# Order of copies and background transfers in the gate stage of a two-group mixer layer

## The chip, the core and the metric

The kernel runs on one NeuronCore of a Trainium2 chip. The core has a matrix engine (TensorE, PE in the profile; its weight loads are listed apart as PEld), a vector engine (DVE), a scalar engine (ACT), GpSimd (POOL) and SyncE (SP). Each of them works through its own list of instructions in order, and semaphores hold them to each other. Transfers are issued by SP and by POOL, onto two different queues, and run on the same 16 DMA engines. The metric is the device time of one execution in microseconds, the median of several runs.

## What is computed

One layer of a diffusion backbone runs for 128 prompt tokens and for 512 sample tokens; the kernel takes the 640 tokens together. The part that matters here is the gated merge of four branches:

```python
proj = h @ lw['w_in']
y_a = a_b * dwconv3(a_c * a_x, lw['conv_a_w'], lw['conv_a_b'])
...
g_a, g_b, g_c, g_d = jnp.split(jax.nn.sigmoid(h @ lw['w_gate'] + lw['b_gate']), N_BRANCH, axis=-1)
merged = (g_a * (y_a @ lw['w_br_a']) + g_b * (y_b @ lw['w_br_b'])
          + g_c * (y_c @ lw['w_br_c']) + g_d * (y_d @ lw['w_br_d']))
return merged @ lw['w_o'], kh, vh, s_f, s_b
```

Here `h` is 640 x 1024, each `y` is 640 x 256, and `merged` is 640 x 1024. Around it stand the input projection, an HGRN scan, neighbourhood attention and a gMLP before, and the output projection, a second norm and a convolutional feed-forward (1024 to 5632, and 2816 back to 1024) behind.

## The kernel before, in words

Everything is float32. A product in float32 is made of three products of a rounded type: each operand is split into a high part (an ACT copy that rounds) and a low part (a DVE subtraction of the high part from the original), and high x high, high x low and low x high are added up in PSUM. So each weight tile and each operand needs a copy on ACT and a subtraction on DVE before the matrix engine can use it.

The gate stage takes 16 *pairs*, numbered 0 to 15 (`p_`): four branches in the order d, a, b, c, with four output tiles each. A pair covers two output tiles of 128 features and all 640 tokens in two halves of 320. It is computed as a two-by-two block product with seven products instead of eight (numbers 1 to 7), so sums of weight blocks and of operand blocks are needed as well. `gprod` issues one of the seven for the gate (12 matmuls), and `bprod` one for the branch (3 matmuls): 105 matmuls of 128x128 by 128x320 in a pair. What a pair needs beside them:

- Weight units `A`, `B`, `C`, `Z` (tiles `w`, `B`, `S` in the profile): `g_a`/`g_al`, `g_b`, `g_c`, `g_zh`/`g_zl` make their high and low parts. `B` is made from the sums in `gx["S"]`, which is half of the region `D`. For pairs 0 to 2 these sums were made by earlier transfers and lie in memory as `gsum`; `g_s01` loads them (`D<-gsum`, on POOL). From pair 3 on `g_s01` adds them on DVE.
- Banks of PSUM (`m`, one bank; `g`, two banks): product 1 lands in one bank and is copied to another on ACT, since two products build on it (`oact(b3, b1)` in `g_pair`, and `oact(p3_, p1_)` for the branch). The sums of the seven products are put together on ACT and DVE in the tiles `ga`, `gb` and `y`, and the gate goes through a sigmoid on ACT (`g_sig`).
- The branch operand `y`: in the second pair of a branch (pairs 1, 5, 9; `n0 == 1`) `y_load` brings the next branch's operand into `gx["Y"]`, the other half of region `D`: SP loads the high part, and POOL adds the low part by an accumulating transfer, which must wait for the first one. At the end of the same pair `y_sums` makes the operand sums from it on DVE (four subtractions and additions, `D<-D`), and `y_split` splits these in the branch's first pair. The operand is `ydd` for branch d, the tile `A` for branch a, and `ybd` and `ycd` in memory for branches b and c.

The order of the gate stage is written out by hand: while `fixed[0]` is set, the engines take `ovec`, `oact`, `opool` and `omm` instructions in the order of the source. What stands before that (input projection, attention) is placed by a scheduler.

Branch a's operand is finished in `evac_in`, in the last tile of the input projection, as half of the tile `YA` (`MG` in the profile). `split_y("A", ...)` splits it there: one ACT copy and one DVE subtraction of 128x1280.

Background transfers: `down_sums` is a list of 72 steps, each one transfer on POOL (`usum`, then `wsum`), which make sums of feed-forward weights in memory, many of them accumulating. `g_all` issues 5 of them ahead of each pair. POOL's list is in order, so a step issued ahead of a pair stands ahead of that pair's `D<-gsum`, of its accumulating transfer for `y`, and of the loads of finished operands (`E<-ybd`, `A<-ycd`).

Of the kernel before, what the change touches and what calls it, by code (L numbers as in the profile page):

```python
# [10 lines left out]
F32R = mybir.dt.float32r  # L11
U8 = mybir.dt.uint8
AF = mybir.ActivationFunctionType
# [3 lines left out]
P = 128  # L17
# [29 lines left out]
T = 640  # L47
# [22 lines left out]
def tile_step(ctx: ExitStack, tc: tile.TileContext, a: dict, outs: list, dbg=None):  # L70
# [58 lines left out]
    def region(tag, shape, dt=F32):  # L129
        return big.tile(shape, dt, tag=tag, name=nm(tag))  # L130
# [25 lines left out]
    ovec, opool, oact = Ordered(nc.vector), Ordered(nc.gpsimd), Ordered(nc.scalar).activation  # L156
# [51 lines left out]
    for x in LORD.split():  # L208
        if x[0] == "w":
            i, h = int(x[1]), int(x[2])  # L210
# [180 lines left out]
    R = {}  # L391
# [6 lines left out]
    def evac_in(sec, n, ps):  # L398
        psv = None if isinstance(ps, list) else ps[:, :, 0:HC]
        if sec in ("ff", "fb"):  # L400
            d = 0 if sec == "ff" else 1
            ff = need("A", "FF", [P, 2, 2, T])
            kk = need("B", "KK", [P, 2, 2, T])
            if psv is None:
                for c in range(2):
                    cs = slice(c * HC, (c + 1) * HC)
                    act(ff[:, d, n, cs], ps[c], AF.Sigmoid)
                    act(kk[:, d, n, cs], ps[c], AF.Sigmoid, scale=-1.0)
            else:
                act(c2(ff[:, d, n]), psv, AF.Sigmoid)  # L410
                act(c2(kk[:, d, n]), psv, AF.Sigmoid, scale=-1.0)
            i = d * 2 + n
            vec.tensor_scalar(ff[:, d, n], ff[:, d, n], oml[:, i:i + 1], lb[:, i:i + 1],
                              ALU.mult, ALU.add)
            vec.tensor_scalar(kk[:, d, n], kk[:, d, n], oml[:, i:i + 1], None, ALU.mult)
        elif sec == "q":
            dd = need("D", "HD", [P, 2560])
            act(c2(dd[:, n * T:(n + 1) * T]), psv, AF.Silu)
        elif sec == "g":
            o = need("MG1", "HO", [P, 2560])  # L420
            act(c2(o[:, 1280 + n * T:1280 + (n + 1) * T]), psv, AF.Silu)
        elif sec == "du":
            x0 = need("X0", "DX0", [P, 2560])
            act(c2(x0[:, n * T:(n + 1) * T]), psv, AF.Copy)
        elif sec in ("ac", "ax", "ab"):
            if (sec, n) == ("ac", 0):
                drain(lambda: "hgrn_out" in R)
            y = need("MG0", "YA", [P, 2, 2, T])
            if sec == "ac":
                act(c2(y[:, 0, n]), psv, AF.Copy)  # L430
                return
            if sec == "ab":
                drain(lambda: "conv" in R)
            x = y[:, 0 if sec == "ax" else 1, n]
            vec.tensor_tensor(c2(x), psv, c2(x), ALU.mult)
            if (sec, n) == ("ab", 1):
                drain(lambda: "ada39" in R)
                R["ya"] = split_y("A", y[:, 1].rearrange("p n t -> p (n t)"))
        elif sec in ("ck", "cq", "cv"):
            if sec == "cv":  # L440
                dst = need("G", "CG", [P, 1280])[:, n * T:(n + 1) * T]
            else:
                f = need("F", "CF", [P, 2560])
                o = 0 if sec == "ck" else 1280
                dst = f[:, o + n * T:o + (n + 1) * T]
            sc = 0.125 if sec == "cq" else 1.0
            cg, cw = (4, 16) if sec == "cq" else (8, 8)
            dv = dst[:, 0:TS].rearrange("p (g r c) -> p r g c", g=cg, r=8)
            for (b, r0, r1) in ((0, 0, 5), (1, 5, 8)):
                src = ps[:, b, 0:(r1 - r0) * 64].rearrange("p (r g c) -> p r g c", g=cg, c=cw)  # L450
                act(dv[:, r0:r1], src, AF.Copy, scale=sc)
            act(dst[:, TS:T], ps[:, 1, 192:320], AF.Copy, scale=sc)
# [220 lines left out]
    def split_y(tag, y):  # L673
        w = region(tag, [P, 2, 2, T], F32R)
        wf = w.rearrange("p h k t -> p h (k t)")
        act(wf[:, 0], y, AF.Copy)
        vec.tensor_tensor(wf[:, 1], y, wf[:, 0].bitcast(F32), ALU.subtract)
        return w
# [472 lines left out]
    def low(w, x, h):  # L1151
        ovec.tensor_tensor(w, x, h.bitcast(F32), ALU.subtract)
# [25 lines left out]
    def g_b(p_, lows=None):  # L1178
        b = gw[p_, "B"] = gunit(p_, 1)
        oact(b[:, 0], gx["S"], AF.Copy)  # L1180
        if lows is None:
            low(b[:, 1], gx["S"], b[:, 0])
        else:
            lows.append((b[:, 1], gx["S"], b[:, 0]))
# [23 lines left out]
    def gprod(o, p_, i, first):  # L1208
        u, n = GPROD[i]
        w = gw[p_, u]  # L1210
        xh_, xl_ = gx["x"][i]
        for k in range(4):
            for j, (h, x) in enumerate(((0, xh_), (0, xl_), (1, xh_))):
                omm(o, w[:, h, n, k, :], x[:, k, :], start=(first and k == 0 and j == 0),
                   stop=(k == 3 and j == 2), skip_group_check=True)
            tick(0.44)
# [19 lines left out]
    def g_sig(p_, i, o, x):  # L1236
        bi, n = gp_id(p_)
        gc = C_BG + GI[BR[bi]] * 8 + n + 4 * i
        oact(o, x, AF.Sigmoid, bias=p1[:, gc:gc + 1])
# [24 lines left out]
    def g_pair0(r):  # L1264
        gx["bi"] = 0
        bank = [pm() for i in range(4)]
        R["mo"] = bank[2]
        b1, b3, b2, b4 = [m[:, 0:HC] for m in bank]
        ga = gw[0, "gt", 0] = gp.tile([P, T], F32, tag="gt", name=nm("ga"))
        gb = gw[0, "gt", 1] = gp.tile([P, T], F32, tag="gt", name=nm("gb"))  # L1270
        ps = gw[0, "ps"] = pg()
        p1_, p3_ = ps[:, 1, 0:HC], ps[:, 0, 0:HC]
        gprod(b1, 0, 1, True)
        oact(ga[:, 0:HC], b1, AF.Copy)
        bprod(p1_, 0, 1, True)
        oact(p3_, p1_, AF.Copy)
        gprod(b3, 0, 2, True)
        ovec.tensor_tensor(ga[:, 0:HC], b3, ga[:, 0:HC], ALU.add)
        g_sig(0, 0, ga[:, 0:HC], ga[:, 0:HC])
        bprod(p3_, 0, 2, False)  # L1280
        drain(lambda: "Y1" in gx)
        gprod(b4, 0, 4, True)
        g_split(3, gx["t3"])
        g_s01(1, r[1])
        gprod(b1, 0, 6, False)
        oact(gb[:, 0:HC], b1, AF.Copy)
        g_a(1, r[1])
        y_sums()
        gprod(b2, 0, 5, True)
        ovec.tensor_tensor(gb[:, 0:HC], b2, gb[:, 0:HC], ALU.subtract)  # L1290
        gx["C"] = region("MG1", [P, 2, 3, HC], F32R)
        lows, x3 = y_split()
        oact(x3[2], x3[1], AF.Copy)
        gprod(b1, 0, 7, False)
        oact(gb[:, HC:T], b1, AF.Copy)
        for x in lows + [x3]:
            low(*x)
        ovec.tensor_tensor(ga[:, HC:T], b4, gb[:, HC:T], ALU.add)
        g_sig(0, 0, ga[:, HC:T], ga[:, HC:T])
        ovec.tensor_tensor(gb[:, HC:T], b2, gb[:, HC:T], ALU.subtract)  # L1300
        r[2] = gp_load(2)
        gprod(b3, 0, 3, True)
        g_al(1, r[1])
        y = gw[0, "y"] = gp.tile([P, T], F32, tag="gt", name=nm("y"))
        c2_ = gw[0, "b2"] = pm()[:, 0:HC]
        bprod(p1_, 0, 6, False)
        oact(y[:, 0:HC], p1_, AF.Copy)
        ovec.tensor_tensor(gb[:, 0:HC], b3, gb[:, 0:HC], ALU.add)
        bprod(c2_, 0, 5, True)
        bprod(p1_, 0, 7, False)  # L1310
        oact(y[:, HC:T], p1_, AF.Copy)
        ovec.tensor_tensor(y[:, HC:T], c2_, y[:, HC:T], ALU.subtract)
        g_s23(1, r[1])
        gx["Y"] = gx["Y1"]

    def g_pair(p_, r):
        n, q = p_ + 1, p_ - 1
# [18 lines left out]
            g_zl(p_, r[p_])  # L1336
        gprod(b1, p_, 1, True)
        g_sig(q, 1, gw[q, "gt", 1], gw[q, "gt", 1])
        oact(b3, b1, AF.Copy)
        g_close(q)  # L1340
        ps = gw[p_, "ps"] = pg()
# [1 line left out]
        bprod(p1_, p_, 1, True)  # L1343
        oact(p3_, p1_, AF.Copy)
        if not q:
            g_b(p_)
            late = g_c(p_, r[p_])
            g_zh(p_, r[p_])
        g_merges(q)
# [29 lines left out]
        y = gw[p_, "y"] = gp.tile([P, T], F32, tag="gt", name=nm("y"))  # L1379
# [42 lines left out]
    def g_all(r):  # L1422
        drain(lambda: "gx3" in R and "last" in R)
        r[1] = gp_load(1)
        fixed[0] = True
        sums_ = down_sums()
        g_pair0(r)
        for p_ in range(1, GPAIR + 1):
            for _ in range(5):
                next(sums_, None)  # L1430
            if p_ == GPAIR:
                fixed[0] = False
                for j in range(GATES + 1, GATES + 3):
                    ld[j] = units[j][0]()
                    rd[j] = units[j][1](ld[j])
            g_pair(p_, r)
        m_split(2)
        m_split(3)
# [1216 lines left out]
```

## Time and profile before

| what | us |
|---|---|
| median of 3 runs | 999.44 |
| lowest and highest run | 998.62, 1199.35 |
| the profiled execution, whole | 999.27 |
| its span, first to last instruction | 997.5 |
| pair 1 begins, pair 15 ends (about) | 290, 524 |

The prediction is made against the profiled execution, 999.27 us. Its span is 997.5 us, so 1.77 us lie around the span. It is 0.17 us below the median of the three runs.

How rows are read. A row of the timeline has the start in us, the duration in us, the engine, the line, the operation, output<-input by the program's names, partitions x elements, and a count where equal instructions follow each other (then the duration is that of the group); in brackets stands the time that the engine had been idle before, and what released it. Most calls in the gate stage go through the helper at line 150, so a line tells little and the tile names tell more. SPq and POOLq rows are issues of transfers. A row of the list of transfers has the size of one in KB and the time from issue to landing in us. A row of the waits has the engine and what it waited for, the total in us, the number of times and the longest. A row of the windows has, for each engine, busy time and in brackets the number of instructions, then the granted clock of TensorE, the DMA engines' busy share and GB/s.

### The profile page before, as it was taken

To read this page: it belongs to the slowest core of one execution; us is meant where nothing else is said; L and a number is where in the kernel's file an instruction comes from. 1 tells how busy PE (TensorE), PEld (TensorE's weight loads), DVE (VectorE), ACT (ScalarE), POOL (GpSimd) and SP (SyncE) were. 2 spreads that over 40 slices of the span, in tenths; PEclk is the share of its full clock that TensorE was granted. 3 is DMA by queue.
4 is the path that set the end of the run, shared out by engine and by line. 5 is a ranking of instruction groups with operands and counts; after the bars stand their busy time and mean duration, and the time that the engine had idled before them with its cause. 6 is when DMAs were issued, how large, how long until landed. Compare 5 with 4: busy or idle time off the path is not lost.

```text
span 997.5 us, 19012 instructions
## 1 busy us (share of the span) xinstructions
PE 984.5 (99%) x7437; PEld 931.6 (93%) x7437; DVE 861.9 (86%) x1411; ACT 592.5 (59%) x1034; POOL 199.9 (20%) x272
## 2 busy tenths in 40 slices
PE   8999999999999999999999999999999999999997
PEld 6899999999989999999998899999999999888886
DVE  6679899878978789888877788999999998999796
ACT  6652343445575565555655376877777777756672
POOL 1000023414123131333200021222222222100004
PEclk9999999999999999999999999999999999999999
DMA  9886349898189799999939785766666666976742
GB/s 356 334 287 245 124 139 299 217 261 275 54 274 259 200 291 268 251 287 301 229 138 349 261 301 156 216 167 169 176 169 163 177 170 193 362 256 230 279 134 105
DMA packets 76858, 227.54 MB, mean 228 GB/s; under 512 B 10561, under 2 KB 25441, under 8 KB 74081
## 3 DMA queue, kind: packets, MB, share of 16 engines
q1 hardware_dynamic: 44832, 149.91, 42.1%
q0 software_dynamic: 31936, 76.43, 32.5%
q8 instruction: 58, 0.95, 0.4%
q14 instruction: 32, 0.25, 0.1%
HBM read 185.26 MB, written 61.36 MB: 247 GB/s over the span
## 4 chain that ended last, share of the span: by engine, by line
PE 85%; DVE 6%; DMA 5%; issue 1%; ACT 1%; POOL 1%; SPq 0%; POOLq 0%; DVEq 0%
PE g L1723 21%; PE m L150 20%; PE m L2186 9%; PE g L374 9%; PE m L1723 5%; PE g L150 4%; PE m L1475 4%; PE g L2186 4%; PE g L955 2%; PE g L1475 1%; PE m L539 1%; DMA D<-hdr 1%; PE m L1718 1%; DMA D<-ycd 1%; DMA ybd<-D 1%
## 5 line engine op out<-in xcount | busy, mean ns | idle before, releaser
L374 PE MATMUL g<-XH,w 128*128 128x320 f32 x576 | 140.5, 318 | 0.0
L374 PEld LDWEIGHTS g<-XH,w 128*128 128x128 f32 x576 | 98.7, 188 | 2.3 <-issue 1.0
L150 PE MATMUL m<-XH,w 128*128 128x320 f32 x416 | 98.9, 311 | 1.1 <-ACT gb L150 0.6
L374 PE MATMUL g<-XL,w 128*128 128x320 f32 x288 | 89.1, 309 | 0.0
L150 PEld LDWEIGHTS m<-XH,w 128*128 128x128 f32 x416 | 70.8, 188 | 3.1 <-ACT gb L150 0.8
L150 PE MATMUL m<-XL,w 128*128 128x320 f32 x208 | 63.0, 310 | 0.0
L2186 PE MATMUL m<-w,XH 128*128 128x512 f32 x246 | 58.5, 390 | 0.0
L2186 PEld LDWEIGHTS m<-w,XH 128*128 128x128 f32 x246 | 46.1, 188 | 9.5
L374 PEld LDWEIGHTS g<-XL,w 128*128 128x128 f32 x288 | 54.2, 188 | 0.3 <-issue 0.2
L150 ACT ACTIVATE w<-raw 128x640 fp32r<-128x640 f32 (+3 forms) x53 | 48.6, 931 | 2.6 <-DMA raw<-in_w_in_dram 1.5
L150 DVE TENSOR_TENSOR w<-raw,w 128x640 fp32r<-128x640 f32 (+3 forms) x47 | 48.5, 1048 | 1.9 <-ACT w L150 1.9
L150 POOL DMA_DIRECT2D wsum<-in_w_dn_dram x36 | 37.2, 1215 | 48.7 <-issue 34.2
L150 DVE SCALAR_TENSOR_TENSOR X<-MG,p2t,X 128x641 f32<-128x641 f32 x44 | 38.9, 883 | 1.0 <-ACT X L150 0.2
L150 DVE SCALAR_TENSOR_TENSOR X<-X,p2t,X 128x641 f32<-128x641 f32 x44 | 38.9, 884 | 0.9
L150 PEld LDWEIGHTS m<-XL,w 128*128 128x128 f32 x208 | 38.6, 188 | 0.6 <-issue 0.6
L1723 PE MATMUL g<-XL,w 128*128 128x320 f32 x240 | 38.6, 310 | 0.0
L1723 PE MATMUL g<-XL,C 128*128 128x320 f32 x240 | 38.3, 309 | 0.0
L150 ACT ACTIVATE gb<-m 128x320 f32<-128x320 f32 x32 | 14.0, 436 | 40.7 <-PE m L150 40.7
L1723 PEld LDWEIGHTS g<-XL,w 128*128 128x128 f32 x240 | 36.0, 188 | 0.6 <-ACT MG L150 0.3
L1723 PEld LDWEIGHTS g<-XL,C 128*128 128x128 f32 x240 | 36.0, 188 | 0.0
L150 ACT ACTIVATE X<-X,p2t 128x641 f32<-128x641 f32 x22 | 20.4, 927 | 18.4 <-DVE X L150 18.4
L150 ACT ACTIVATE X<-g 128x320 f32<-128x320 f32 x30 | 13.1, 437 | 30.6 <-PE g L1723 30.6
(622 smaller groups left out, 2946.3 us busy)
## 6 DMA issues: line engine op xcount, KB each, us to landing
wsum<-in_w_dn_dram POOLq DMA_DIRECT2D x30, 512.0 KB, 12.4
raw<-in_w_gp_dram SPq DMA_DIRECT2D x23, 640.0 KB, 7.7
raw<-in_w_up_dram SPq DMA_DIRECT2D x28, 512.0 KB, 5.3
raw<-in_w_in_dram SPq DMA_DIRECT2D x19, 512.0 KB, 6.0
H<-in_w_adt_dram SPq DMA_DIRECT2D x19, 512.0 KB, 4.6
G<-in_w_up_dram SPq DMA_DIRECT2D x12, 512.0 KB, 5.1
raw<-wsum SPq DMA_DIRECT2D x12, 512.0 KB, 5.5
actx<-X POOLq DMA_DIRECT2D x22, 256.0 KB, 4.4
```

What stands on the lines that cost most here:

```text
L150: r = f(*args, **kw)
L374: mm(o, w[:, h, k0 + k, :], r(k)[:, s], start=(k == 0 and i == 0), stop=(k == kt - 1 and i == 2))
L539: mm(m[W * g:W * g + W, (i - s0) * W:(i - s0 + 1) * W], lhs, rhs, start=True, stop=True, tile_position=(64 * par, W * g))
L955: mm(o, x(kx)[:, ts], w[:, h, k, :], start=(kx == 0 and i == 0), stop=(kx == 7 and i == 2))
L1475: mm(m, mh[MHN[q]][:, hx, k % 2, t * P:(t + 1) * P], wo[q][:, hw, k % 2, :], start=(k == 0 and i == 0), stop=(k == 7 and i == 2))
L1718: mm(o, w[:, k, :], x[:, k, :], start=(first and not part and k == 0 and j == 0), stop=(part == 1 and k == 3), skip_group_check=True)
L1723: z = mm(o, w[:, k, :], x[:, k, :], start=(first and k == 0 and j == 0), stop=(k == 3 and j == 2), skip_group_check=True)
L2186: mm(ps, s[t // 4][:, hx, k, o:o + P], w[:, hw, k, c0:c1], start=first, stop=i == 2 and bi == len(batch) - 1 and k == len(ks) - 1, skip_gr ...
```

## The change

```diff
@@ evac_in @@
             if (sec, n) == ("ab", 1):
                 drain(lambda: "ada39" in R)
-                R["ya"] = split_y("A", y[:, 1].rearrange("p n t -> p (n t)"))
+                R["yv"] = y[:, 1].rearrange("p n t -> p (n t)")
@@ g_pair0 @@
         oact(ga[:, 0:HC], b1, AF.Copy)
         bprod(p1_, 0, 1, True)
         oact(p3_, p1_, AF.Copy)
+        ya = R["ya"] = region("A", [P, 2, 2, T], F32R)
+        ya = ya.rearrange("p h k t -> p h (k t)")
+        oact(ya[:, 0], R["yv"], AF.Copy)
+        low(ya[:, 1], R["yv"], ya[:, 0])
         gprod(b3, 0, 2, True)
         ovec.tensor_tensor(ga[:, 0:HC], b3, ga[:, 0:HC], ALU.add)
@@ g_pair @@
         gprod(b1, p_, 1, True)
         g_sig(q, 1, gw[q, "gt", 1], gw[q, "gt", 1])
+        if not q:
+            g_b(p_)
         oact(b3, b1, AF.Copy)
         g_close(q)
 ...
         bprod(p1_, p_, 1, True)
         oact(p3_, p1_, AF.Copy)
         if not q:
-            g_b(p_)
             late = g_c(p_, r[p_])
             g_zh(p_, r[p_])
@@ g_all @@
         for p_ in range(1, GPAIR + 1):
-            for _ in range(5):
+            for _ in range(2 if p_ % 4 == 1 else 6):
                 next(sums_, None)
```

It has three parts. The split of branch a's operand moves from the end of the input projection into pair 0, behind the two copies of product 1. In pair 1 (`q` is 0 only there) the split of unit `B` moves ahead of the bank copy `b3<-b1`. And of the background steps, 2 instead of 5 are issued ahead of pairs 1, 5, 9 and 13, and 6 instead of 5 ahead of the others. Up to pairs 4, 8, 12 and 16 the sum is the same, and all 72 are issued by pair 15 in both.

The order of the instructions on PE and on DVE is the same as before. On ACT two places differ. In pair 0, the last copy of the weights of pair 0 (`B<-raw`), the copy of the operand (`A<-MG`), the copies of product 1 (`ga<-m`, `g<-g`) and the sigmoid stand before as follows:

```order
L150 ACTIVATE B_3585<-raw_3064 128x640
L676 ACTIVATE A_3594<-MG_274_2952 128x1280
L150 ACTIVATE ga_3606<-m_3602 128x320
L150 ACTIVATE g_3608<-g_3608 128x320
L150 ACT_TABLE_LOAD
L150 ACTIVATE ga_3606<-ga_3606,cst 128x320
```

and now, on ACT at the same place, so:

```order
L150 ACTIVATE B_3585<-raw_3064 128x640
L150 ACTIVATE ga_3603<-m_3599 128x320
L150 ACTIVATE g_3605<-g_3605 128x320
L150 ACTIVATE A_3623<-MG_274_2952 128x1280
L150 ACT_TABLE_LOAD
L150 ACTIVATE ga_3603<-ga_3603,cst 128x320
```

The copy of 128x1280 has moved behind the two copies that empty PSUM banks. In pair 1, ACT has before, from the sigmoid of pair 0's second gate (`gb<-gb`) to the copy of unit `C` (`w<-raw`), with `w<-D` as the high part of unit `B` and `m<-m` as the copy `b3<-b1`:

```order
L150 ACTIVATE gb_3607<-gb_3607,cst 128x640
L150 ACTIVATE m_3757<-m_3756 128x320
L150 ACTIVATE g_3780<-g_3780 128x320
L150 ACTIVATE w_3785<-D_2907 128x1280
L150 ACTIVATE w_3788<-raw_3597 128x640
```

and now, on ACT in pair 1:

```order
L150 ACTIVATE gb_3604<-gb_3604,cst 128x640
L150 ACTIVATE w_3770<-D_2907 128x1280
L150 ACTIVATE m_3754<-m_3753 128x320
L150 ACTIVATE g_3780<-g_3780 128x320
L150 ACTIVATE w_3785<-raw_3594 128x640
```

`w<-D` has moved up past two copies. POOL's queue around pairs 8 to 10 has before, with `A<-ycd` as the load of the finished operand for branch c and `D<-ycd` as the accumulating transfer of pair 9:

```order
L1255 DMA A_4900<-ycd 128x2560
L150 DMA wsum<-in_w_dn_dram 128x4x256 x5
L150 DMA D_2907<-ycd 128x1280
L150 DMA wsum<-in_w_dn_dram 128x4x256
L150 DMA wsum<-in_w_dn_dram 128x2x256 x2
```

and now, on POOL at the same place:

```order
L1255 DMA A_4900<-ycd 128x2560
L150 DMA wsum<-in_w_dn_dram 128x4x256 x2
L150 DMA D_2907<-ycd 128x1280
L150 DMA wsum<-in_w_dn_dram 128x4x256 x4
L150 DMA wsum<-in_w_dn_dram 128x2x256 x2
```

Three background transfers have moved from ahead of `D<-ycd` to behind it. The same holds for `D<-ybd` in pair 5 (two `usum` and one `wsum`) and for `D<-A` in pair 1 (three `usum`).

## Prediction

> **What bounds the kernel now.** I read the page's busy times first, then TensorE's waits from pair 0 to the end of the gate stage (278 to 527 us), then the windows, to see where matmuls are missing.
>
> ```profile
> PE 984.5 (99%) x7437; PEld 931.6 (93%) x7437; DVE 861.9 (86%) x1411; ACT 592.5 (59%) x1034; POOL 199.9 (20%) x272
> ...
> PE m L150 <- DVE w L150: 1.0, 1, 1.0
> PE m L150 <- ACT gb L150: 0.6, 1, 0.6
> PE m L150 <- DVE gb L150: 0.5, 1, 0.5
> PE g L150 <- ACT g L150: 0.2, 1, 0.2
> ...
> 280.00:300.00 20.00, 18.95 (x126) 18.13 (x125) 14.89 (x24) 13.43 (x22) 7.34 (x14) 1.00 1.00 332
> ...
> 420.00:440.00 20.00, 20.00 (x138) 20.00 (x138) 17.61 (x25) 9.54 (x16) 7.69 (x10) 1.00 1.12 283
> 440.00:460.00 20.00, 18.91 (x127) 18.39 (x126) 18.56 (x24) 11.89 (x19) 7.56 (x8) 1.00 1.11 282
> ```
>
> TensorE is busy 99% of the span at full clock, and in the gate stage only four of its waits show. The change removes no matmul, so all it can win is these waits. A full window has 138 matmuls in 20 us. 280 to 300 us is short of 12 and 440 to 460 us of 11. The steady spacing follows from product 7 of pair 1, below: 12 matmuls in 1.76 us (298.52 to 300.28), 0.147 us each. So about 1.8 and 1.6 us are missing there. A wait costs somewhat more than its row in the waits, since the pipeline refills; so I take losses from start to start. The ceiling of a gain is about 4 us, 0.4% of the time. Less than 2% either way counts as no change here, and nothing in these numbers comes near 2%.
>
> **Part 1, the split of branch a's operand (pair 0).**
>
> ```profile
> 276.97 1.26 ACT L676 ACTIVATE A<-MG 128x1280 fp32r<-128x1280 f32 x1
> 278.40 0.31 PE L150 MATMUL m<-XH,w 128*128 128x320 f32 x1
> 278.45 0.44 ACT L150 ACTIVATE g<-g 128x320 f32<-128x320 f32 x1
> 278.77 1.48 DVE L677 TENSOR_TENSOR A<-MG,A 128x1280 fp32r<-128x1280 f32 x1
> 278.94 0.70 PE L150 MATMUL g<-E,w 128*128 128x320 f32 x3 [0.23 <-ACT g L150]
> 279.48 0.31 PE L150 MATMUL m<-XH,B 128*128 128x320 f32 x1
> 288.31 0.56 ACT L150 ACTIVATE ga<-ga,cst 128x320 f32<-128x320 f32 x1 [1.05 <-DVE ga L150]
> 288.92 0.44 ACT L150 ACTIVATE y<-g 128x320 f32<-128x320 f32 x1
> 289.41 0.45 PEld L150 LDWEIGHTS g<-MG,S 128*128 128x128 f32 x3 [0.35 <-ACT y L150]
> ```
>
> The 1.26 us copy delays the copy `g<-g`, and the branch's product 2 waits for it. The matmul at 278.40 would be followed at 278.55, and the three matmuls of the branch by 278.99; the next product starts at 279.48, so 0.49 us are lost. With the copy behind, `g<-g` follows `ga<-m` and is out by about 277.7: this wait goes.
>
> It comes back 10 us later. The weight load at 289.41, and the matmul with it, hangs on ACT's `y<-g`, which follows the sigmoid at 288.31, which waits for DVE. DVE's order is unchanged. Its subtraction `A<-MG,A` starts at 278.77; now the copy ends about 278.9 (276.97, plus two copies at a spacing near 0.33, plus 1.26), so the subtraction starts about 0.15 later, and `ga`, the sigmoid and what follows move with it. TensorE arrives 0.49 earlier and waits longer for a chain that is no earlier. Bounds: all 0.49 is kept if `y<-g` was really held by TensorE alone; 0.15 is lost if all of the chain is. `y<-g` starts 0.05 after the sigmoid's end, so I take the nearer end: **+0.1 us**. Other work that moves is hidden: pair 1's SP load of the operand is issued at 280.28, 1.4 us behind the copy's new end.
>
> **Part 2, unit B ahead of the bank copy (pair 1).**
>
> ```profile
> 284.24 0.54 POOL L150 DMA_DIRECT2D D<-gsum  x1 [5.97 <-DVE XL L150]
> D<-gsum POOLq DMA_DIRECT2D x1, 640.0 KB, 6.3
> ...
> 290.63 0.83 ACT L150 ACTIVATE gb<-gb,cst 128x640 f32<-128x640 f32 x1
> 292.01 0.42 ACT L150 ACTIVATE m<-m 128x320 f32<-128x320 f32 x1 [0.55 <-PE m L150]
> 293.13 0.31 PE L150 MATMUL m<-XH,w 128*128 128x320 f32 x1
> 294.96 1.49 DVE L150 TENSOR_TENSOR w<-D,w 128x1280 fp32r<-128x1280 f32 x1 [3.11 <-ACT w L150]
> 294.98 0.56 PE L150 MATMUL m<-F,w 128*128 128x320 f32 x2
> 296.51 1.73 PE L150 MATMUL m<-F,w 128*128 128x320 f32 x10 [0.97 <-DVE w L150]
> 298.08 0.60 PE L150 MATMUL g<-E,w 128*128 128x320 f32 x3
> 298.52 1.92 PE L150 MATMUL m<-X,w 128*128 128x320 f32 x12
> ```
>
> Product 6 starts at 294.98, and its third matmul needs the low part of `B`, which DVE ends at 296.45. DVE stood idle 3.11 us before, waiting for ACT's `w<-D`, a copy of the size of `A<-MG` above. The 12 matmuls take 298.08 - 294.98 = 3.10 us instead of 1.76, a loss of 1.34, and they started 0.09 late (12 x 0.147 after 293.13 is 294.89): 1.43 us. Now `w<-D` starts when the sigmoid ends, about 291.4; its sums landed at 284.24 + 6.3 = 290.5. With 1.26 us it ends at 292.7, DVE ends the low part at 294.2, 0.7 us before the product that needs it. The wait goes whole.
>
> Behind `w<-D` now stand ACT's copies `m<-m` and `g<-g`. `m<-m` would end near 292.95 to 293.1, and product 2 at 293.13 builds on that bank: between no wait and 0.1; I take 0.05 lost. `g<-g` waited for TensorE until 293.33 anyway. The C and Z copies and DVE's subtractions behind them come more than 1 us earlier, as TensorE does, and the next `D<-gsum` on POOL too, since it waits for the low part. Sum of part 2: **-1.4 us**.
>
> **Part 3, background transfers (pairs 1, 5, 9).** Only pair 9 shows a wait for them.
>
> ```profile
> 414.99 0.33 SPq L1094 DMA_DIRECT2D D<-ycd  x1
> D<-ycd SPq DMA_DIRECT2D x1, 640.0 KB, 6.6
> 422.13 0.90 POOL L150 DMA_DIRECT2D D<-ycd  x1 [4.59 <-DVE C L150]
> D<-ycd POOLq DMA_DIRECT2D x1, 640.0 KB, 10.2
> wsum<-in_w_dn_dram POOLq DMA_DIRECT2D x3, 512.0 KB, 12.8
> 359.34 0.92 POOL L150 DMA_DIRECT2D D<-ybd  x1 [9.41 <-DVE gb L150]
> D<-ybd POOLq DMA_DIRECT2D x1, 640.0 KB, 6.2
> ...
> 432.32 2.07 DVE L150 TENSOR_TENSOR D<-D 128x320 f32<-128x320 f32 x4 [1.55 <-DMA D<-ycd]
> 441.09 0.60 PE L150 MATMUL m<-MG,w 128*128 128x320 f32 x3
> 442.26 0.42 PE L150 MATMUL m<-XH,w 128*128 128x320 f32 x1 [0.57 <-ACT gb L150]
> 444.12 0.60 PE L150 MATMUL g<-MG,S 128*128 128x320 f32 x3
> 445.24 0.42 PE L150 MATMUL m<-XH,w 128*128 128x320 f32 x1 [0.52 <-DVE gb L150]
> ```
>
> The accumulating transfer lands at 432.3, DVE has then waited 1.55 us, and DVE's list reaches the subtraction and ACT's copy that TensorE needs in pair 10 too late. The matmul behind 441.09 was due at 441.53 and came at 442.26, that behind 444.12 at 444.56 and came at 445.24: 0.73 + 0.68, with some 0.1 of refill each 1.6 us, as the missing 11 matmuls say. Pairs 2 and 6, with the same work on time, show no wait, so nothing else is late there.
>
> Now two `wsum` transfers stand between `A<-ycd` and `D<-ycd`, not five. They are issued near 402 and, at 12.8 us, are gone by 416. In pair 5 the same kind of transfer, with nothing issued on POOL for 9.4 us ahead of it, took 6.2 us. TensorE and all it drives is then 1.3 us earlier, so SP's half is issued at 413.7 and lands at 420.3, POOL issues near 420.8 (0.5 behind, as now), and it lands at 427.0 by the row of `D<-ybd` and at 431.0 by its own old row. DVE is ready at 432.32 - 1.55 - 1.3 = 429.5. By the first nothing is lost, by the second all of the 1.6 stays. I take the first, since what set the second stood ahead in the queue. **-1.6 us.**
>
> The Trainium skill ("DMA: Bandwidth & Descriptors", Queues, rings and completion order) says that a DMA engine takes one queue's descriptors in ring order and turns between queues by packets. [...]
>
> Costs of part 3: six steps instead of five elsewhere. POOL has room:
>
> ```profile
> 518.27 1.09 POOL L1465 DMA_DIRECT2D X<-in_x_sample_dram  x2 [22.51 <-PE m L150]
> ```
>
> POOL ends the steps early enough to stand 22.5 us idle near the end of the stage, and ahead of pairs 4, 8, 12, 16 the count is the same as before. I put it at nothing; without that cover a late operand costs what pair 9 shows, up to 1.6.
>
> **Sum.** 999.27 + 0.1 - 1.4 - 1.6 = 996.4. Behind the gate stage TensorE has no wait in the list, so the gain should reach the end.
>
> **Rivals.**
> - The transfer of pair 9 still lands late (its old 10.2 us, or POOL's own backlog from the sixes ahead of pairs 6 to 8). Then 1.6 stays: 998.0. For it: DMA engines are over-full at 420 to 440 (1.12). Against: pair 5's row. 0.13.
> - Part 1 keeps its 0.49, because `y<-g` was held by TensorE: 995.8. 0.12.
> - The six steps ahead of other pairs make one operand or weight late there: up to 1.6 given back, 996.4 to 998.0. No row shows such a wait today. 0.09.
> - Slower: `w<-D` now stands ahead of `m<-m` on ACT, and it waits for `D<-gsum`. If that lands late, the bank copy and product 2 wait too. From a landing near 291.4 each us costs TensorE about one; part 2 is used up at 292.8, and the whole change at about 294.4, 10.1 us after the issue. With the 10.2 us of `D<-ycd` it would be 999.4; with the 12.8 of a `wsum`, 1001.9. Against: it took 6.3 with five `usum` transfers right behind it, now two. 0.03.
> - The change does nothing measurable in any part (all waits replaced): 999.3. 0.02.
>
> **How the numbers follow.** The forecast, both waits gone and part 1 near zero, has 0.61. The range 995.3 to 998.4 takes in the second to fourth case and a few tenths between runs (998.62 to 999.44 among the two near runs before); the slower cases are left out. Faster by over 2% (below 979) or slower by over 2% (above 1019) needs 20 us, which no row offers: 0.01 each, same 0.98.
>
> **What would show it.** Right: no TensorE wait for `w` in pair 1; `w<-D` at about 291.4 and DVE's idle time before `w<-D,w` below 1 us; `D<-ycd` (POOL) landing in under 7.5 us, DVE `D<-D` of pair 9 without an idle time for it, and no waits for `gb` near 440. Part 1: no wait for `g` at 278.9, and a longer one at 289.4. Wrong: a new wait for `m<-m` in pair 1, a wait for a transfer in pairs 2 to 12, or the gain lost to a wait behind 525 us.

## The result and the profile after

| | kernel before | changed kernel |
|---|---|---|
| median, us (16 runs of each) | 999.04 | 996.78 |
| the profiled execution, us | 999.27 | 997.16 |
| its span, us | 997.5 | 995.3 |

The ratio of the times is 0.9979, with an interval of 0.9971 to 0.9987: 2.1 us less, between 1.3 and 2.9. Three single runs, one of the kernel before (1199.35 us) and one each of e3 and e13 below (1608.04 and 1371.69), were slow as a whole, and the ratios leave them out. That is a real gain, and far below the 2% from which a change counts here. The forecast was 996.4, in a range of 995.3 to 998.4.

The two profiled executions are cut at two instructions that both kernels have: POOL's issue `ycd<-C`, which lies just ahead of the changed order, and the first matmul of the output projection. The first two rows are from the timeline of the kernel before:

```profile
277.68 0.59 POOL L150 DMA_DIRECT2D ycd<-C  x1 [20.92 <-DVE C L889]
524.55 0.63 PE L1475 MATMUL m<-w,E 128*128 128x512 f32 x2
```

and these from that of the changed kernel:

```profile
278.17 0.59 POOL L150 DMA_DIRECT2D ycd<-C  x1 [20.93 <-DVE C L889]
522.18 0.63 PE L1480 MATMUL m<-w,E 128*128 128x512 f32 x2
```

The stretch between them is 246.87 us before and 244.01 after: 2.86 us shorter. The forecast of its terms was 2.9. The profiled execution itself is only 2.11 shorter, since the changed kernel came to the stretch 0.49 later; over the profiles of this study that start lies between 277.6 (e12) and 278.7 (e11), and these two have the same instructions ahead of it, so 0.49 is within the spread between executions. Behind the stretch nothing differs between these two (473.0 and 473.1 us to the end of the span). The stretch of before varies too: in a second profile of that kernel (e12) it is 246.52.

TensorE's busy time on the page, its waits in the gate stage, and the windows of the changed kernel:

```profile
PE 983.9 (99%) x7437; PEld 932.0 (94%) x7437; DVE 862.3 (87%) x1411; ACT 592.2 (59%) x1034; POOL 198.9 (20%) x272
```

```profile
PE g L150 <- ACT y L150: 0.6, 1, 0.6
```

```profile
280.00:300.00 20.00, 19.39 (x131) 18.87 (x130) 17.11 (x25) 13.67 (x22) 6.99 (x11) 1.00 0.99 322
...
440.00:460.00 20.00, 20.00 (x139) 20.00 (x138) 17.78 (x24) 12.59 (x21) 5.79 (x6) 1.00 1.12 302
```

The four waits of before are gone from the list; the one that it has now is in pair 0, at product 7 of the branch, where before a weight load waited 0.35 us. The window from 440 is full again (139 matmuls, before 127); that from 280 has 131 instead of 126. Some 5 of the 7 still missing are this wait (0.77 us, start to start), and one is a weight load at 290.93 that waits 0.27 us for DVE's low part of pair 1's weights (0.17, start to start).

Part 2 did in pair 1 what was forecast. The timeline there, ACT, DVE, PE and POOL rows of the changed kernel in order of time:

```profile
292.05 1.25 ACT L150 ACTIVATE w<-D 128x1280 fp32r<-128x1280 f32 x1
293.21 0.42 ACT L150 ACTIVATE m<-m 128x320 f32<-128x320 f32 x1
293.33 1.49 DVE L150 TENSOR_TENSOR w<-D,w 128x1280 fp32r<-128x1280 f32 x1 [0.92 <-ACT w L150]
293.82 0.31 PE L150 MATMUL m<-XH,w 128*128 128x320 f32 x1
295.12 0.56 POOL L150 DMA_DIRECT2D D<-gsum  x1 [4.09 <-DVE w L150]
295.58 1.92 PE L150 MATMUL m<-F,w 128*128 128x320 f32 x12
300.20 1.28 ACT L150 ACTIVATE w<-D 128x1280 fp32r<-128x1280 f32 x1 [1.96 <-DMA D<-gsum]
301.50 0.44 ACT L150 ACTIVATE gb<-m 128x320 f32<-128x320 f32 x1
```

The copy `w<-D` now runs right behind the sigmoid, which starts at 291.31 and takes 0.83; DVE stands idle 0.92 us for it instead of 3.11, and the low part ends at 294.82, 0.76 ahead of the product 6 that needs it (0.7 was forecast). Product 6 runs its 12 matmuls without a gap, and `m<-m` behind the copy delays nothing. The last two rows are pair 2's unit `B`, and the experiments turn on them.

In pair 9 the operand is in time. The timeline of the changed kernel for SP's half, POOL's accumulating half and DVE's sums:

```profile
414.24 0.33 SPq L1094 DMA_DIRECT2D D<-ycd  x1
418.72 0.93 POOL L150 DMA_DIRECT2D D<-ycd  x1 [13.31 <-DMA D<-ycd]
429.94 2.06 DVE L150 TENSOR_TENSOR D<-D 128x320 f32<-128x320 f32 x4
```

and its list of transfers, for pair 2's sums and for the two halves of pair 9's operand:

```profile
D<-gsum POOLq DMA_DIRECT2D x1, 640.0 KB, 5.0
...
D<-ycd SPq DMA_DIRECT2D x1, 640.0 KB, 3.9
...
D<-ycd POOLq DMA_DIRECT2D x1, 640.0 KB, 9.6
```

DVE no longer waits. But it is SP's half that became fast (6.6 before, 3.9 now); the accumulating half still takes 9.6 us, and lands in time because it is issued 3.4 us earlier, of which SP's half gives 2.7 and its earlier issue 0.7.

### The profile page after: what moved, and what is told of

It is laid out like the page before. It is cut to its first block, busy times and chain, and to the rows that moved or that the text cites. A ratio compares the mean times of both kernels' runs of the same rounds, so it can differ in the third digit from the quotient of the medians.

```text
span 995.3 us, 19011 instructions
## 1 busy us (share of the span) xinstructions
PE 983.9 (99%) x7437; PEld 932.0 (94%) x7437; DVE 862.3 (87%) x1411; ACT 592.2 (59%) x1034; POOL 198.9 (20%) x272
## 4 chain that ended last, share of the span: by engine, by line
PE 93%; DVE 3%; DMA 2%; POOL 1%; issue 1%; ACT 0%; SPq 0%; POOLq 0%
PE m L150 22%; PE g L1728 21%; PE g L374 12%; PE m L2191 9%; PE m L1728 5%; PE g L150 5%; PE m L1480 4%; PE g L2191 4%; PE g L955 2%; PE g L1480 1%; PE m L539 1%; PE m L1723 1%; DMA A<-in_w_ada_dram 1%; PE m L882 1%; POOL hss L317 1%
```

## The experiments

Two theories were tried against each other. By the first, that of the prediction, each part stands alone: part 2 wins the wait in pair 1, part 3 wins the wait in pair 9, part 1 nothing. By the second, part 2 only moves pair 1's wait on to pair 2, unless the transfer of pair 2's sums (`D<-gsum`) also comes earlier, and it is part 3's entry for pair 1 that makes it so. Whether the landings of one profile stand for all runs, a second profile of the kernel before (e12) tests.

The table holds all results, as the ratio to the kernel before with its interval. The times of the kernel before were 998.80, 998.52 and 998.71 us in the three groups of runs. "Steps ahead" is the number of background transfers between the previous load of sums and the operand's accumulating transfer `D<-A`, and (after the plus) between `D<-A` and pair 2's `D<-gsum`. The landings, in us from the start of the span, are start of the issue plus time to landing, from the timeline and the list of transfers. "Lost near 301 to 305" is TensorE's gap, start to start, at the first matmul that needs ACT's `gb<-m`.

| kernel | us | ratio | steps ahead | `D<-A` landed | `D<-gsum` issued, landed | lost near 301 to 305 |
|---|---|---|---|---|---|---|
| before (profile) | 999.04 | | 5+0 | 299.46 | 296.75, 301.05 | 0 |
| e12, before, second profile | 998.83 (one run) | | 5+0 | 299.55 | 296.68, 301.18 | 0.10 |
| e1, part 1 alone | 999.10 | 1.0004 [0.9996, 1.0012] | 5+0 | 299.60 | 296.96, 301.16 | 0 |
| e2, part 2 alone | 1000.80 | 1.0014 [1.0005, 1.0022] | 5+0 | 299.30 | 294.44, 301.51 | 1.74 |
| e11, part 2, second profile | 1001.18 (one run) | | 5+0 | 301.11 | 295.50, 303.00 | 2.18 |
| e10, part 2 and pair 9's steps | 1000.10 | 1.0011 [1.0002, 1.0020] | 5+0 | 300.08 | 294.61, 302.31 | 2.32 |
| e3, part 3 alone | 998.00 | 0.9993 [0.9984, 1.0002] | 2+0 | 298.38 | 296.91, 301.21 | 0 |
| e4, parts 2 and 3 | 996.45 | 0.9978 [0.9969, 0.9986] | 2+0 | 296.82 | 294.54, 299.74 | 0 |
| e9, part 2 and pair 1's steps | 996.64 | 0.9981 [0.9972, 0.9990] | 2+0 | 296.93 | 294.62, 299.82 | 0 |
| changed kernel | 996.78 | 0.9979 [0.9971, 0.9987] | 2+0 | 297.11 | 295.12, 300.12 | 0 |
| e5, steps behind, order else as before | 1000.00 | 1.0016 [1.0007, 1.0025] | 0+5 | 295.97 | 296.83, 303.03 | 1.80 |
| e13, part 2, pair 1's steps behind | 996.55 | 0.9978 [0.9969, 0.9987] | 0+0 | 296.43 | 295.46, 299.76 | 0 |

**e1: part 1 alone.** The first two hunks of the diff, in `evac_in` and `g_pair0`:

```diff
-                R["ya"] = split_y("A", y[:, 1].rearrange("p n t -> p (n t)"))
+                R["yv"] = y[:, 1].rearrange("p n t -> p (n t)")
...
+        oact(ya[:, 0], R["yv"], AF.Copy)
+        low(ya[:, 1], R["yv"], ya[:, 0])
```

> The kernel before, with the first part of the change alone (the split of branch a's operand in pair 0). Theory: TensorE's wait for g near 278.9 us (0.5 us from start to start) goes and comes back at the branch's product 7 near 289.4, since ACT's y copy hangs on a DVE chain that is no earlier; the time is that of before within 0.2 us. The loss at 289.4 grows from 0.35 to 0.8 or more. Rival: the y copy was held by TensorE alone; then 0.5 us are won and the loss at 289.4 stays at 0.35. The waits near 295 and 440 stay in both cases.

No measurable difference. TensorE's timeline of e1 at the two places:

```profile
278.56 0.60 PE L150 MATMUL g<-E,w 128*128 128x320 f32 x3
...
289.46 0.70 PE L150 MATMUL g<-MG,S 128*128 128x320 f32 x3 [0.61 <-ACT y L150]
```

The first row carries no wait any more, and product 7 of the branch starts at 289.46 against 289.41 before: TensorE reached the place earlier and stood longer. So the 0.49 is given back whole, and 0.05 with it; at 290.47 another 0.18 goes, where a weight load waits for DVE's low part of pair 1's weights. The waits near 440, expected to stay, are not there (see e12).

**e2: part 2 alone.**

```diff
         g_sig(q, 1, gw[q, "gt", 1], gw[q, "gt", 1])
+        if not q:
+            g_b(p_)
         oact(b3, b1, AF.Copy)
...
         if not q:
-            g_b(p_)
             late = g_c(p_, r[p_])
```

> The kernel before, with the second part alone (unit B ahead of the bank copy in pair 1). Theory: the wait of TensorE for DVE's low part in pair 1 (1.4 us) goes, no wait for the bank copy over 0.1 us comes, and 1.4 us are won at the end. Rival: pair 9's transfer is bound to the background transfers' own time, not to TensorE's; then TensorE meets it 1.4 us earlier, the waits near 440 grow from 1.6 to 3.0 us, and nothing is won.

Slower than before, by 0.05 to 0.22%, where 1.4 us were to be won. The wait for the low part of `B` is gone, as in the changed kernel, but a new one stands 8 us later. First the new row in TensorE's waits in the gate stage of e2, then two pieces of its chain of waits (start, length, what), then ACT's timeline:

```profile
PE m L150 <- ACT gb L150: 1.6, 1, 1.6
```

```profile
294.44 7.07 DMA D<-gsum
...
303.24 2.04 PE m L150 x12
```

```profile
301.59 1.27 ACT L150 ACTIVATE w<-D 128x1280 fp32r<-128x1280 f32 x1 [4.03 <-DMA D<-gsum]
302.77 0.42 ACT L150 ACTIVATE gb<-m 128x320 f32<-128x320 f32 x1
```

`D<-gsum` was issued 2.3 us earlier than before and landed 0.5 us later: it took 7.1 us instead of 4.3. ACT's copy of pair 2's `B` waits for it, and behind that copy in ACT's list stands `gb<-m`, which TensorE needs before its next product. The kernel before has the same two rows, with TensorE's first matmul behind them:

```profile
301.18 1.28 ACT L150 ACTIVATE w<-D 128x1280 fp32r<-128x1280 f32 x1 [2.41 <-DMA D<-gsum]
302.36 0.42 ACT L150 ACTIVATE gb<-m 128x320 f32<-128x320 f32 x1
...
302.92 0.32 PE L150 MATMUL m<-XH,w 128*128 128x320 f32 x1
```

In e2 the matmul starts 0.47 us after the start of `gb<-m`. By that, before, it could have started at 302.83: it had 0.09 us of slack, and no wait shows. A TensorE that is 1.43 us earlier, with sums that land no earlier, must lose 1.34 there; with sums 0.46 later (301.51 against 301.05), 1.80. The gap of e2 is 1.74. So the wait is not won but moved.

**e3: part 3 alone**, and **e4: parts 2 and 3** (all but part 1).

```diff
-            for _ in range(5):
+            for _ in range(2 if p_ % 4 == 1 else 6):
```

> The kernel before, with the third part alone (2 background steps ahead of pairs 1, 5, 9, 13 and 6 ahead of the others). Theory: the accumulating transfer of pair 9 lands in under 7.5 us instead of 10.2, DVE does not wait for it, the two waits near 440 go, and 1.6 us are won. Rival: the sixes make something else late; then a new wait of TensorE or DVE for a transfer shows in pairs 2 to 12, and less than 1 us is won.

> The changed kernel without its first part (the operand's split stays at the end of the input projection). Theory: the first part is worth nothing, so the time is that of the changed kernel within 0.2 us, about 2.3 to 2.9 us under before, with waits at 278.9 (0.5) and 289.4 (0.35) and none behind. Rival: the first part is worth its 0.5 us; then this is 0.5 us slower than the changed kernel. A third way: the first part costs some tenths, since the DVE chain starts 0.15 later; then this is 0.1 to 0.5 us faster.

Part 3 alone may be worth 0.7 us, but the interval includes zero. The waits near 440 are gone in e3; the landing under 7.5 us (8.2 measured) and the 1.6 us were missed. Alone, part 2 costs 1.4 and part 3 brings 0.7; together they bring 2.2 [1.4 to 3.1], as much as the whole change. They are no sum: part 2 needs part 3.

**e5: the order on the queue, not the number of steps.** The kernel before with its five steps per pair; in pairs 1, 5 and 9 they are issued behind the operand's transfers instead of ahead.

```diff
-            for _ in range(5):
-                next(sums_, None)
+            gx["steps"] = lambda: [next(sums_, None) for _ in range(5)]
+            if p_ % 4 != 1 or p_ == 13:
+                gx["steps"]()
...
             y_load(bi + 1)
+            gx["steps"]()
```

> The kernel before, still with five background steps for each pair, but those of pairs 1, 5 and 9 issued behind the two transfers of the branch operand instead of ahead of them. Nothing else differs. Theory (order on the queue): what stands ahead of the accumulating transfer sets its landing; in pair 9 it lands in under 7.5 us with five steps right behind it, the waits near 440 go, and the median is that of the third part alone, about 998.0, 0.8 under before. Rival (number of transfers in flight): it still lands in 8.5 us or more, and the median is that of before, 998.8.

That was missed: it is slower. Pair 9's waits are gone, though its accumulating half took 8.5 us, as by the rival, and not under 7.5. But the steps of pair 1 now stand between `D<-A` and pair 2's sums. The list of transfers of e5, for these two:

```profile
D<-A POOLq DMA_DIRECT2D x1, 640.0 KB, 6.3
...
D<-gsum POOLq DMA_DIRECT2D x1, 640.0 KB, 6.2
```

and TensorE's timeline behind them:

```profile
304.80 0.42 PE L150 MATMUL m<-XH,w 128*128 128x320 f32 x1 [1.64 <-ACT gb L150]
```

Without steps ahead, `D<-A` took 6.3 us instead of 9.9; with five ahead, `D<-gsum` took 6.2 instead of 4.3. ACT's order is that of the kernel before, so the new wait comes from the landing alone.

**e9, e10, e11: which entry of part 3 carries the gain.** All have part 2. e9 takes part 3's two steps for pair 1 only, e10 for pair 9 only, and e11 is e2 again.

```diff
-            for _ in range(5):
+            for _ in range({1: 2, 2: 8}.get(p_, 5)):
```

for e9, and with `{9: 2, 10: 8}` for e10.

> The second part (unit B first in pair 1) with fewer background steps ahead of pair 1 alone: 2 there, 8 ahead of pair 2, 5 elsewhere. The second part alone met a new wait of 1.7 us near 301 us, where ACT's copy for pair 2 stood ahead of a bank copy and waited for the sums of pair 2 to land. Theory: the steps ahead in pair 1 set that landing; with 2 it comes near 299.7 instead of 301.5, the wait goes, and pair 9's wait is all that is left: about 997.5 to 999. Rival: the second part alone was slow (1000.8) because of pair 9; then this stays near 1000.5 with 2.5 us or more of waits near 440.

> The second part with fewer background steps ahead of pair 9 alone: 2 there, 8 ahead of pair 10, 5 elsewhere. Theory: the new wait near 301 us stays at 1.5 to 2 us, the waits near 440 go, and the median comes near 998 to 998.5 (before, less the 0.8 of the third part, and nothing won by the second). Rival (pair 9 alone made the second part slow): near 996.8, as fast as the whole change.

> The second part alone once more, for a second profile: its first profile was of its fastest run (998.2) and showed 1.7 us lost near 301 and nothing near 440, while its median was 1000.8. Theory: the typical run has waits of 2 to 3 us near 440 on top of the one near 301, since pair 9's transfer keeps its own time while TensorE comes earlier or not. Rival: the wait near 301 itself grows to 4 us in the typical run and nothing shows near 440.

The wait near 301 decides. e9 is as fast as the whole change, and faster than expected. e10 is no better than e2, and misses the 998 to 998.5 expected of it; a row of TensorE's waits in the gate stage, and one of its list of transfers:

```profile
PE m L150 <- ACT gb L150: 2.2, 1, 2.2
```

```profile
D<-gsum POOLq DMA_DIRECT2D x1, 640.0 KB, 7.7
```

Near 440 e11 shows no wait, and e9 a gap of 0.14 us only, although both issue five steps ahead of pair 9. So both accounts of e11 failed: no waits near 440, and 2.2 us, not 4, near 301.

The moved wait can cost more than its gap. In e11 the stretch took 247.64 us, in e2 245.70; the gaps account for 0.44 of these 1.94 us. The rest is TensorE's clock. The windows of e11 behind the gap (the third figure from the right is the granted clock):

```profile
304.00:306.00 2.00, 1.27 (x7) 1.27 (x8) 1.61 (x2) 2.00 (x5) 0.02 (x1) 0.90 1.07 316
306.00:308.00 2.00, 2.00 (x9) 2.00 (x9) 1.75 (x3) 0.63 (x2) 0.79 (x1) 0.50 1.07 315
308.00:310.00 2.00, 2.00 (x12) 2.00 (x11) 0.49 (x1) 1.22 (x3) 0.56 (x1) 0.74 1.10 239
```

A full window of 2 us has 15 or 16 matmuls; here there are 9 and 12, so about 10 of 0.147 us are missing: 1.5 us. In the profiles of e2 and e10 the clock stays at 1.00 behind gaps of 1.74 and 2.32. The times of e2 fall into two groups, four from 998.2 to 999.1 and eight from 1000.0 to 1001.8, and those of e10 likewise (four from 998.5 to 998.8, seven from 999.6 to 1000.7). A drop of the clock in some executions and not in others would make such groups, but it was seen in one profile only. The profile of e10 speaks against it as the only cause: it is of one of the seven (999.59 us), with no drop behind its gap, and 0.6 us of its time are a wait of TensorE for DVE's `gcol` at line 303, behind the stretch, which the profiles of e7 and e13 also have (1.1 and 0.3) and no other has. So what makes the groups stays open.

**e13: part 2, with all five steps of pair 1, but behind `D<-gsum` of pair 2.** As many steps as in e2, one place later.

```diff
             g_s01(n, r[n])
+            gx["steps"]()
...
-            for _ in range(5):
-                next(sums_, None)
+            gx["steps"] = lambda: [next(sums_, None) for _ in range(5)]
+            if p_ != 1:
+                gx["steps"]()
```

> The second part (unit B first in pair 1) with five background steps for each pair as before; only those of pair 1 are issued behind the load of pair 2's sums instead of ahead of it. Theory (order on the queue): nothing but the operand's transfer stands ahead of that load, it lands in about 5 us or less (7.1 to 7.7 with the steps ahead), the wait of 1.7 to 2.3 us near 301 is gone, and the median is near 996.6, as with 2 steps ahead. Rival (number of transfers in flight): ten steps run beside the load, it lands in 7 us or more, the wait stays, and the median is near 1000.

As fast as the whole change. The list of transfers of e13:

```profile
D<-A POOLq DMA_DIRECT2D x1, 640.0 KB, 5.8
...
D<-gsum POOLq DMA_DIRECT2D x1, 640.0 KB, 4.3
```

Between e2, e5 and e13 only the place of the five steps on the queue differs for these two transfers (e5 lacks part 2, so its issue is later): what stands ahead is paid for, what stands behind is not.

**e7 and e8: can part 1 be made to pay?** Both are the whole change with the operand's split placed elsewhere. In e7 the DVE subtraction goes behind the addition to `ga`; in e8 the ACT copy goes behind the copy of `XH`, and the subtraction behind the low part of pair 1's unit `A`.

```diff
-        low(ya[:, 1], R["yv"], ya[:, 0])
         gprod(b3, 0, 2, True)
         ovec.tensor_tensor(ga[:, 0:HC], b3, ga[:, 0:HC], ALU.add)
+        low(ya[:, 1], R["yv"], ya[:, 0])
```

for e7, and for e8

```diff
-        oact(ya[:, 0], R["yv"], AF.Copy)
-        low(ya[:, 1], R["yv"], ya[:, 0])
...
+        oact(h_, gx["t3"], AF.Copy)
+        oact(ya[:, 0], R["yv"], AF.Copy)
...
         g_al(1, r[1])
+        low(ya[:, 1], R["yv"], ya[:, 0])
```

> The whole change, and in pair 0 DVE's low part of branch a's operand behind the addition that the first sigmoid waits for instead of ahead of it. Theory: the chain of DVE and ACT that ends in the y copy starts 0.6 us earlier (then held by the table load), the loss at the branch's product 7 falls from 0.87 to about 0.35 us, and the median falls by 0.5 to about 996.2. Rival: the chain is held by ACT's copies further on, and the loss stays at 0.8.

> The whole change, with the copy of branch a's operand on ACT behind the copy of operand 3, and its low part on DVE behind pair 1's first low part. Theory: the chain starts 1.4 us earlier, the y copy is held by TensorE alone, the loss at product 7 falls from 0.87 to 0.35 us, and the median falls by 0.5 to about 996.2. Rival: the late low part holds up the operand's accumulating transfer on POOL and with it the sums of pair 2 behind it on the queue; then a wait near 301 us comes back and the median is above 997.5.

e7: 996.63, 0.9979 [0.9970, 0.9988]; e8: 997.09, 0.9983 [0.9974, 0.9992]. Neither differs from the changed kernel by more than the intervals, so the 0.5 us expected of each were missed. In both, the gap at product 7 in pair 0 falls from 0.77 to 0.25 us, and about half or more of that is lost again. In e7 a gap of 0.25 opens at 301.58, where `gb<-m` (301.11) waits behind pair 2's `w<-D`; so the changed kernel has little slack there. In e8 it is lost at pair 1's bank copy, by DVE's, ACT's and TensorE's timelines:

```profile
289.11 1.49 DVE L150 TENSOR_TENSOR A<-MG,A 128x1280 fp32r<-128x1280 f32 x1
```

```profile
292.93 0.42 ACT L150 ACTIVATE m<-m 128x320 f32<-128x320 f32 x1
```

```profile
293.39 0.42 PE L150 MATMUL m<-XH,w 128*128 128x320 f32 x1 [0.61 <-ACT m L150]
```

The subtraction at 289.11 makes DVE's sums for `gb`, and so the sigmoid, `w<-D` and `m<-m`, late: a gap of 0.77 us for one of 0.52 removed.

**e12: the kernel before once more.** No edit.

> The kernel before, unchanged, for a second profile of it. Theory: the wait near 440 differs from run to run with the landing of pair 9's accumulating transfer (10.2 us in the first profile, 8.3 to 9.0 in four kernels that leave it as it is); below about 8.7 us there is no wait. So this profile shows 0 to 1.6 us there, and its time is lower by about what is missing. Rival: the kernel before always has 1.6 us there.

The accumulating transfer of pair 9 took 9.3 us here, not 10.2. DVE's and TensorE's timelines of e12:

```profile
431.89 2.07 DVE L150 TENSOR_TENSOR D<-D 128x320 f32<-128x320 f32 x4 [1.00 <-DMA D<-ycd]
```

```profile
444.80 0.42 PE L150 MATMUL m<-XH,w 128*128 128x320 f32 x1 [0.53 <-DVE gb L150]
```

TensorE loses 0.18 and 0.68 us, 0.86 together, instead of 1.41 by the same count; the wait for ACT's `gb` is not in its list. (The further 0.10 in the table is a weight load in pair 2 that waits for ACT's `gb<-m`.) In e1, which has all five steps ahead of pair 9 and the same order there, the transfer took 8.7 us, DVE's row has no wait, and TensorE loses nothing:

```profile
431.04 2.07 DVE L150 TENSOR_TENSOR D<-D 128x320 f32<-128x320 f32 x4
```

## Why the prediction came out right, and which steps did not hold

**The sum: right, and in part by luck.** The stretch became 2.86 us shorter for a forecast of 2.9 (+0.1, -1.4, -1.6), and nothing behind it took that back. Against the stretch of e12 it is 2.51 shorter; the median fell by 2.26 us. The luck is twofold: part 2 was won only through an effect of part 3 that the prediction did not count, and part 3's own term was read from the profile with the latest landing of all (10.2 us, against 8.3 to 9.3 in the six others with five steps ahead).

**Part 1, +0.1: right, if a little small.** From `ycd<-C` to the matmul behind the two waits, the kernel before takes 12.57 us (to 290.25) and the changed kernel 12.76 (to 290.93): 0.2 lost. The changed kernel's chain of waits through pair 0 shows the way on which it is given back:

```profile
278.22 1.19 ACT A L150
...
279.44 1.49 DVE A L150
280.93 0.41 DVE ga L150
...
288.99 0.56 ACT ga L150
289.55 0.33 ACT y L150
...
289.93 0.71 PE g L150 x3
```

From the operand's copy on, ACT and DVE are the path, not TensorE. The copy and its subtraction are on that path wherever they stand in this stretch; moving them frees TensorE at one end and makes it wait at the other. e1 measured it alone, and e4, which leaves part 1 out, is no slower than the whole change.

**Part 2, -1.4: the right size, but not by itself.** The step that failed is "the next `D<-gsum` on POOL" comes earlier, "since it waits for the low part". Its issue came earlier, its landing did not: in e2 it was issued 2.3 us earlier and landed 0.5 later. The prediction looked no further than the issue, and did not ask when the sums are needed, although the kernel before shows ACT idle 2.41 us for them at 301.18 and TensorE with 0.09 us to spare. The term came true because part 3 lets `D<-A`, the transfer ahead on the same queue, end at 297.1 instead of 299.5. The prediction priced part 3 in pair 9 alone, so that was luck.

The slower rival (a `D<-gsum` that holds ACT's list, and with it a bank copy) had the right mechanism at the wrong pair. At pair 1's own sums it did not happen, as the row of `w<-D` at 292.05 shows; at pair 2's it did, in e2, e10 and e11. There it took all of part 2 (1.74 us for 1.43 in e2's profile) and, in e11, where the clock fell behind the wait, more. How much of e2's loss in the other runs is the clock is not shown.

**Part 3, -1.6: mis-sized and put in the wrong place.** "Only pair 9 shows a wait for them" was true of the profile and false of the worth. In pair 9 the wait is worth what the landing of that execution makes it: 1.41 (1.6 with the refill) at 10.2 us, 0.86 at 9.3, nothing in e1 at 8.7. e3 measured 0.7 us for part 3 alone, in an interval from 0.2 lost to 1.6 won; the term of 1.6 lies at its far end. Added to part 2 the same table is worth 4.35 us between the medians (e2 at 1000.80, e4 at 996.45) and 3.6 by the ratios, nearly all of it through pair 1: e9, without pair 9's entry, is as fast.

Against the one profile of before the terms hold, since its pair 9 was at the late end. Against the median, 1.43 + 0.86 = 2.3 is nearer to the 2.26 measured.

**Part 3, how it works in pair 9: wrong half.** The prediction had the accumulating half fall from 10.2 to 6.2 us (under 7.5) and SP's half stay at 6.6. Measured: 9.6 and 3.9. With two steps ahead, SP's half took 3.9 to 4.1 us in all six kernels, and 4.0 with none (e5); with five, 6.3 to 6.9 in all seven. The accumulating half took 8.0 to 9.6 with two, 8.5 with none and 8.3 to 10.2 with five: it does not follow the steps ahead of it. What holds it at 8 and more stays open.

The shares of the two queues from 414.3 to 418.2 us show the reason. Kernel before, then changed kernel (packets, MB, share of the 16 engines' time):

```profile
q0 software_dynamic: 646, 0.64, 112.1%
q1 hardware_dynamic: 13, 0.07, 4.5%
```

```profile
q1 hardware_dynamic: 171, 0.79, 75.8%
q0 software_dynamic: 53, 0.05, 8.2%
```

SP's half was issued at 414.99 before and at 414.24 after, so the kernel before has 0.7 us less of it in this window. Over the same 3.9 us from its issue (to 418.9) its hardware queue moved 44 packets, 15.5%, beside 559 of the software queue, 99.0%. Before, the fourth and fifth `wsum` (issued at 413.67 and 416.31) fill the engines while SP's half stands in its queue. After, both `wsum` have landed by about 416.5 (the second was issued at 404.15 and took 12.3 us), and SP's half has the engines nearly alone. The prediction itself had the two `wsum` "gone by 416", and still left SP's half at 6.6.

The step that failed here is SP's half: the prediction had it take its old 6.6 us (413.7 to 420.3) and gave all of the shortening to the accumulating half. The Trainium skill ("DMA: Bandwidth & Descriptors", Queues, rings and completion order) says that an engine turns between the queues that it has work for, by packets. Turns do not show here behind a full software queue: in the first 2.5 us from the issue of SP's half, the hardware queue moved one packet in the kernel before and none in e1, e2 and e12, while the software queue moved 410 to 497; in e3 and e4, with two steps ahead, it had moved 26 and 30 within 2.0 us. So SP's half moved next to nothing until the software queue ran low. Whether its packets stood ready before that, no trace here shows. The same section's ring order within one queue agrees with e13 against e5: five steps ahead of `D<-gsum` made 4.3 us into 6.2, and five behind it left 4.3.

**Other rivals.** "Part 1 keeps its 0.49" fell with e1. "Six steps make an operand late elsewhere" does not show: in the gate stage the changed kernel's list has no TensorE wait but the one in pair 0, and e4's only one, also in pair 0.

## What to carry to other kernels

When a wait is removed, look at the next transfer that the freed engine will want, and read how much slack it has from the profile: an earlier issue is no earlier landing when other work stands ahead on the same queue. A wait for a transfer in one profile is one draw of its landing, so take a second profile before giving it a price. Measure the parts of a change in pairs as well as alone: here one part cost 1.4 us alone and won some 1.5 with another, whose own worth could not be told from nothing.

## What was not expected of the hardware

- TensorE stood still for 2.2 us in e11, and for some 3.4 us from about 305.6 on its granted clock was then 0.50; behind the 2.32 us of e10 it was not. The Trainium skill ("TensorE: Matmul & The Clock Gate", Part 1: The HAM clock gate) says that the clock is halved after an idle window of about 3.4 us and full again after a busy one of the same length, at a phase that is not tied to the kernel. The half clock and its length agree with e11; the idle time before it was shorter than that window.
- The same load of 640 KB, `D<-gsum` on the software queue, took 4.2 to 5.6 us where it was issued, with no step between the two, less than 3 us before `D<-A`, the transfer ahead of it, had landed, and 7.1 to 7.7 where it was issued 4.9 to 5.6 us before (e2, e10, e11).
- A load on the hardware queue took 6.3 to 6.9 us while accumulating transfers of 512 KB ran on the software queue, and 3.9 to 4.1 us where these were ending or gone.
- The accumulating transfer `D<-A` took 9.7 to 10.5 us with five steps ahead, 5.9 to 8.7 with two, and 5.8 and 6.3 with none, with the steps right behind it in e5.
